# Storing the low parts of the input projection's weights in the first half and loading them in the second

## The chip, the cores and the metric

One core of a Trainium2 chip runs the whole layer. The metric is the device time of one execution in microseconds. TensorE is called PE here, VectorE DVE, ScalarE ACT, GpSimd POOL and SyncE SP; SP issues nearly all of the kernel's DMA transfers, in the order in which they stand in its queue.

## The reference, cut to what matters

One layer of a hybrid encoder, 1024 rows by 1024 channels in fp32. The input projection has 3088 columns that three groups of heads share; the rest of the layer follows from them.

```python
h = rmsnorm(x, pre_mix_norm[l])
proj = h @ w_in[l]
(a_q, a_k, a_v, s_z, s_xbc, s_dt, g_qkv, g_z, g_b, g_a) = jnp.split(proj, offs, axis=-1)
att = swa_sink_alibi(a_q, a_k, a_v, attn_sinks[l])     # sliding window attention
ssd = ssd_mixer(s_z, s_xbc, s_dt, ...)                 # conv, chunked state space scan
gdn = gdn_mixer(g_qkv, g_z, g_b, g_a, ...)             # conv, chunked delta rule with a triangular solve
mix = jnp.concatenate([att, ssd, gdn], axis=-1) @ w_out[l]
x = x + rmsnorm(mix, post_mix_norm[l])
h = rmsnorm(x, pre_ffn_norm[l])
f = (jax.nn.silu(h @ ffn_w_gate[l]) * (h @ ffn_w_up[l])) @ ffn_w_down[l]
x = x + rmsnorm(f, post_ffn_norm[l])
```

## The kernel before, in words

The 1024 rows are worked on in two halves of 512. Each half of phase 1 computes its input projection, the gated delta rule (`gdn_*`), the state space blocks (`ssd_*`) and attention; the second half also holds the out projection of the first half's rows. Phase 2 does the out projection of the second half and the feed-forward part, which the change doesn't touch.

Every fp32 matrix product is made of three products of rounded operands. A weight piece of 128 x 512 (four blocks of 128 x 128, or two of 128 x 256) is loaded from HBM on SP (`wr`, three buffers), ACT rounds it to `hi` (`wh`, six buffers), and a subtract gives the rest, `lo` = raw - `hi` (`wl`, six buffers). PE then multiplies `hi` by `hi`, `hi` by `lo` and `lo` by `hi` into one PSUM tile. `split_eng` gives the subtracts of phase 1 to POOL and DVE in turn. The same weights are loaded, rounded and subtracted in both halves: 48 pieces of the input projection in each, named after their columns (gz for the gate rows, gk, gq, gv, B, C, x, z, aq, ak, av).

The order on each engine isn't written out: a scheduler in the framework sets it from estimated times and from priorities (the code in `tc.high_priority()` goes ahead where it can), and it is fixed when the program is built. Each engine then runs its list in order, and so does SP: a transfer whose data or buffer isn't ready holds up every transfer behind it. SP's transfers use eight completion semaphores in turn, so each also waits for the one eight before it.

Three places are needed below. At the start, the second half's rows of x (tile `x`, line 291) are loaded early, and ACT (`junk`, line 250) and DVE normalise them between the first matmuls of the gate columns (`mm_gz`) and their evacuation (`gth_gz`, `dtn`, `gz`). In each half DVE inverts a unit triangular matrix per chunk (lines 505 to 550): a loop of 16 steps (`Tpr`, `Tst`, lines 521 and 523), the result stored to HBM (`vd<-Tst`, line 525) and loaded back in another layout (`Tst<-vd`, `Wst<-vd`, lines 527 and 528), then two products of four slices each (lines 534 and 536), stored again (line 541) and loaded as `Vd` (line 554) for the matmuls `lx` (line 573). On the same DVE run the conv steps (line 347), the masks `sE` (line 693), which PE needs for `y` (line 700), and the state `ssd_st` (line 714). At the end of phase 1 attention's rows `o` (lines 902 and 904) are transposed (`tp_f`, line 228) for the out projection.

Of the kernel before, what the change touches and what calls it, by code (L numbers as in the profile page):

```python
# [8 lines left out]
F32 = mybir.dt.float32  # L9
F32R = mybir.dt.float32r  # L10
AF = mybir.ActivationFunctionType
ALU = mybir.AluOpType
# [4 lines left out]
P = 128  # L17
SEQ = 1024
D = 1024
KB = D // P  # L20
# [10 lines left out]
WC = 544  # L31
# [38 lines left out]
def trunk(ctx, tc, a):  # L70
    nc = tc.nc
    dma = nc.sync.dma_start
# [4 lines left out]
    def f32(ap):  # L77
        return ap.bitcast(F32)
# [4 lines left out]
    dpool = ctx.enter_context(tc.tile_pool(name="dpool", bufs=1, space=DRAM))  # L83
# [86 lines left out]
    def split_eng():  # L170
        cnt[0] += 1
        return pool if phase[0] == 1 and cnt[0] % 2 else vec

    def split_piece(name, n, width, hi, lo, fill):

        def v(t):
            return t[:, 0:n * width].rearrange("p (k c) -> p k c", k=n)

        with tc.high_priority():
            raw = wpool.tile([P, WC], F32, tag="wr", name=f"wr_{name}")  # L180
            for dst, src in fill:
                dma(v(raw)[:, :, dst:dst + src.shape[1]], src.rearrange("(k p) c -> p k c", p=P))
            act(out=v(hi), in_=v(raw), func=AF.Copy)  # L183
            split_eng().tensor_tensor(v(lo), v(raw), f32(v(hi)), op=ALU.subtract)  # L184
        return [(v(hi)[:, k], v(lo)[:, k]) for k in range(n)]

    def wpair(name):
        return [wsp.tile([P, WC], F32R, tag=tg, name=f"{tg}_{name}") for tg in ("wh", "wl")]

    def piece(name, srcs, kb, width=P, tiles=None):  # L190

        out = []
        n0 = WC // width
        for k0 in range(0, kb, n0):
            n = min(n0, kb - k0)
            nm = f"{name}{k0}"
            out += split_piece(nm, n, width, *(tiles or wpair)(nm),
                               [(dst, src[k0 * P:(k0 + n) * P]) for dst, src in srcs])
        return out

    def gemm_rows(ps, hl, wp, tsl):

        for k, ((hi, lo), (whi, wlo)) in enumerate(zip(hl, wp)):
            pe.matmul(ps, hi[:, tsl], whi, start=k == 0, stop=False)  # L204
            pe.matmul(ps, hi[:, tsl], wlo, start=False, stop=False)  # L205
            pe.matmul(ps, lo[:, tsl], whi, start=False, stop=k == len(wp) - 1)  # L206

    def gemm(ps, wp, hl):
        for k, ((whi, wlo), (hi, lo)) in enumerate(zip(wp, hl)):
            pe.matmul(ps, whi, hi, start=k == 0, stop=False)  # L210
            pe.matmul(ps, whi, lo, start=False, stop=False)  # L211
            pe.matmul(ps, wlo, hi, start=False, stop=k == len(wp) - 1)  # L212
# [105 lines left out]
        return hT  # L318

    def proj(h, hT, name, parts):  # L320
        wp = piece(f"{name}{h}", parts, KB)
        ps = ps_mm.tile([P, HT], F32, tag="mm", name=f"mm_{name}{h}")
        gemm(ps, wp, hT)
        return ps

    def proj_rows(h, hT, name, parts, width, evac):

        wp = piece(f"{name}{h}", parts, KB, width)
        for t in range(NT):
            ps = ps_mm.tile([P, HT], F32, tag="mm", name=f"mm_{name}{h}{t}")  # L330
            gemm_rows(ps[:, 0:width], hT, wp, slice(t * P, (t + 1) * P))
            evac(t, ps)

    def conv_block(h, hT, name, col, b, out):
        ps = proj(h, hT, name, [(0, w_in[:, col:col + P])])
        cb = cpool.tile([P, HT + 3], F32, tag="cb", name=f"cb_{name}{h}")
        if h == 0:
            pool.memset(cb[:, 0:3], 0.0)
        else:
            pool.tensor_copy(cb[:, 0:3], carry[:, b, :])  # L340
        act(out=cb[:, 3:], in_=ps, func=AF.Copy)
        if h == 0:
            pool.tensor_copy(carry[:, b, :], cb[:, HT:HT + 3])
        u = out
        act(out=u, in_=ps, func=AF.Identity, scale=wconv[:, b, 3:4], bias=wconv[:, b, 4:5])
        for i in (2, 1, 0):
            stt(out=u, in0=cb[:, i:i + HT], scalar=wconv[:, b, i:i + 1], in1=u,
                op0=ALU.mult, op1=ALU.add)
        th = cb[:, 0:HT]
        act(out=th, in_=u, func=AF.Tanh)  # L350
        stt(out=out, in0=th, scalar=1.0, in1=u, op0=ALU.add, op1=ALU.mult)

    def gate_rows(h, hT, name, parts, width, more=None):

        out = [ablk(f"{name}{h}{i}") for i in range(2)]
        tiles = [out[t // 2][:, t % 2 * 256:(t % 2 + 1) * 256] for t in range(NT)]

        def evac(t, ps):
            th = cpool.tile([P, HT + 3], F32, tag="cb", name=f"gth_{name}{h}{t}")[:, 0:256]
            act(out=th, in_=ps[:, 0:256], func=AF.Tanh, scale=0.5)  # L360
            stt(out=tiles[t], in0=th, scalar=1.0, in1=ps[:, 0:256], op0=ALU.add, op1=ALU.mult)
            if more is not None:
                more(t, ps)

        proj_rows(h, hT, name, parts, width, evac)
        return tiles
# [421 lines left out]
    def half(h, hT, order):  # L788
# [35 lines left out]
        def att_blocks():  # L824
            aq = []
            for b in range(2):
                ps = proj(h, hT, f"aq{b}", [(0, w_in[:, b * 64:b * 64 + 64]),
                                            (64, w_in[:, 128 + b * 64:192 + b * 64])])
                aq.append(ablk(f"aq{h}{b}"))
                act(out=aq[b], in_=ps, func=AF.Copy)  # L830
            ps = proj(h, hT, "ak", [(0, cols(O_AK))])
            ak = ablk(f"ak{h}")
            act(out=ak, in_=ps, func=AF.Copy)
            ps = proj(h, hT, "av", [(0, cols(O_AV))])
            avT = cpool.tile([P, HT + 3], F32, tag="cb", name=f"avT{h}")[:, 0:HT]
            act(out=avT, in_=ps, func=AF.Copy)
            ps = mx(f"tp_av{h}")
            for t in range(NT):
                pe.transpose(ps[:, t * P:(t + 1) * P], avT[:, t * P:(t + 1) * P], ident)
            av = ablk(f"av{h}").rearrange("p (t c) -> p t c", t=NT)  # L840
            act(out=av, in_=ps.rearrange("p (t c) -> p t c", t=NT), func=AF.Copy)
            st["att"] = (aq, ak, av)
# [17 lines left out]
    def block_first():  # L860
# [14 lines left out]
        for g in range(ng):  # L875
            c0 = g * gw
            wp = piece(f"wo{h}{g}", [(0, a["w_out"][0][:, c0:c0 + gw])], KB, gw)
            for t in range(NT):
                r0 = h * NT + t
# [221 lines left out]
    for g in range(2):  # L1101
        ps = [mx(f"mm_o1{g}{t}", ("f", ("mm", "tp")[t % 2])[g]) for t in range(NT)]
        if g == 0:
            for t in range(NT):
# [3 lines left out]
        wp = {k: piece(f"wo1{g}{k}", [(0, a["w_out"][0][k * P:(k + 1) * P, g * HT:(g + 1) * HT])], 1, HT)[0]  # L1108
              for k in korder}
# [244 lines left out]
```

## Time and profile before

| | |
|---|---|
| time, median of 3 runs | 1271.78 us (1269.67 to 1272.04) |
| profiled execution, time | 1269.6 us |
| profiled execution, span | 1267.8 us |
| mean granted clock of TensorE | 0.983 |
| busy: PE, DVE, ACT, POOL | 1217.6, 924.2, 573.6, 214.6 us |
| moved by DMA | 168.15 MB; HBM read 126.82, written 40.11 MB |

Times inside the execution count from the span's start. Phase 1's first half runs to about 200 us, its second half to about 560 us. A row of the timeline gives start and duration in us, engine, line, operation and tiles, and in brackets the engine's idle time before it with what ended it. A row of the waits gives the total, the number and the longest.

### The profile page before, as it was taken

Reading aid. Unit: us, or ns where it says so; the run is one execution under the profiler, and the core shown is the slowest. Engines: PE = TensorE matmul, PEld = TensorE weight load, DVE = VectorE, ACT = ScalarE, POOL = GpSimd, SP = SyncE. Lnnn points to the kernel's source line nnn. Section 1 sums busy time; section 2 is a strip of 40 time slices with the busy share of each in tenths; the row PEclk is TensorE's granted clock in tenths of the full one; section 3 lists DMA queues with packets and bytes.
Section 4 is the critical chain, followed back from the end, with each engine's and each line's share of the span. In section 5 each row is a group of like instructions: output and inputs, shape, how many; then the busy total and the mean of one; then the engine's idle time right before and its main releaser. Section 6 shows DMA issues by size and latency. Waiting matters only on the chain.

```text
span 1267.8 us, 18690 instructions
## 1 busy us (share of the span) xinstructions
PE 1217.6 (96%) x6432; PEld 1008.5 (80%) x6432; DVE 924.2 (73%) x1850; ACT 573.6 (45%) x1245; POOL 214.6 (17%) x313
## 2 busy tenths in 40 slices
PE   4999999999998999979999999999999999999997
PEld 4878788887787889867887888888888887888885
DVE  5677875887788585654577999886677767767885
ACT  7454434546444353553456344333333334444661
POOL 3343454333444531200010000000000000000000
PEclk9999999999998999979999999999999999999999
DMA  7323433133332213458263465442333368676315
GB/s 228 97 71 70 91 74 81 53 107 85 82 82 58 87 41 115 127 191 271 77 224 106 159 210 174 160 155 84 125 108 108 106 230 286 184 234 212 96 57 199
DMA packets 181795, 168.15 MB, mean 133 GB/s; under 512 B 52510, under 2 KB 137018, under 8 KB 181700
## 3 DMA queue, kind: packets, MB, share of 16 engines
q1 hardware_dynamic: 164276, 133.14, 35.9%
q10 hardware_dynamic: 17424, 33.82, 7.2%
q8 instruction: 50, 0.82, 0.3%
q14 instruction: 45, 0.37, 0.1%
HBM read 126.82 MB, written 40.11 MB: 132 GB/s over the span
## 4 chain that ended last, share of the span: by engine, by line
PE 81%; DVE 9%; DMA 4%; ACT 2%; issue 2%; SPq 1%; POOL 1%; ACTq 0%; DVEq 0%; POOLq 0%
PE mm_p L1225 5%; PE mm_p L1227 5%; PE mm_p L1226 5%; PE gram L486 1%; PE mm_o L1118 1%; PE mm_o L1119 1%; PE mm_o L1120 1%; PE ao L779 1%; PE mm_o L204 1%; PE y L700 1%; DVE Tpr L534 1%; PE mm_o L205 1%; PE mm_o L206 1%; DMA x<-in_x_dram 1%; DMA wr_e<-in_ffn_w_gate_dram 1%
## 5 line engine op out<-in xcount | busy, mean ns | idle before, releaser
L167 POOL TENSOR_TENSOR rsq<-ssv,mhalf 128x1 f32<-128x1 f32 x32 | 20.8, 654 | 745.0 <-DVE ssv L257 714.8
L183 ACT ACTIVATE wh_wo<-wr_wo 128x512 fp32r<-128x512 f32 x32 | 19.9, 630 | 41.5 <-DMA wr_wo<-in_w_out_dram 16.5
L204 PE MATMUL mm_z<-wh_z,hhi_a 128*128 128x256 f32 x128 | 38.4, 300 | 0.0
L184 DVE TENSOR_TENSOR wl_wo<-wr_wo,wh_wo 128x512 fp32r<-128x512 f32 x24 | 17.6, 733 | 27.9 <-ACT wh_wo L183 27.6
L204 PE MATMUL mm_o<-wh_wo,hhi_m 128*128 128x256 f32 x128 | 37.0, 289 | 0.0
L205 PE MATMUL mm_z<-wl_z,hhi_a 128*128 128x256 f32 x128 | 36.7, 287 | 0.0
L206 PE MATMUL mm_z<-wh_z,hlo_a 128*128 128x256 f32 x128 | 36.6, 286 | 0.0
L205 PE MATMUL mm_o<-wl_wo,hhi_m 128*128 128x256 f32 x128 | 35.7, 280 | 0.0
L206 PE MATMUL mm_o<-wh_wo,hlo_m 128*128 128x256 f32 x128 | 35.7, 280 | 0.0
L1118 PE MATMUL mm_o<-wh_wo,mhi 128*128 128x512 f32 x64 | 25.2, 394 | 1.4 <-ACT mhi L233 1.4
L210 PE MATMUL mm_x<-hhi_a,wh_x 128*128 128x512 f32 x64 | 26.1, 408 | 0.0
L700 PEld LDWEIGHTS y<-xs,sE 128*128 128x128 f32 x128 | 18.9, 201 | 9.0 <-DVE sE L693 7.4
L211 PE MATMUL mm_x<-hlo_a,wh_x 128*128 128x512 f32 x64 | 25.9, 404 | 0.0
L700 PE MATMUL y<-xs,sE 128*128 128x64 f32 x128 | 19.8, 284 | 6.3 <-DVE sE L693 6.3
L212 PE MATMUL mm_x<-hhi_a,wl_x 128*128 128x512 f32 x64 | 25.8, 403 | 0.0
L204 PEld LDWEIGHTS mm_z<-wh_z,hhi_a 128*128 128x128 f32 x128 | 25.3, 197 | 0.6
L1119 PE MATMUL mm_o<-wl_wo,mhi 128*128 128x512 f32 x64 | 25.2, 393 | 0.0
L205 PEld LDWEIGHTS mm_z<-wl_z,hhi_a 128*128 128x128 f32 x128 | 24.9, 195 | 0.3
L206 PEld LDWEIGHTS mm_z<-wh_z,hlo_a 128*128 128x128 f32 x128 | 25.0, 196 | 0.0
L1120 PE MATMUL mm_o<-wh_wo,mlo 128*128 128x512 f32 x64 | 24.5, 396 | 0.0
L204 PEld LDWEIGHTS mm_o<-wh_wo,hhi_m 128*128 128x128 f32 x128 | 24.1, 188 | 0.4 <-issue 0.3
L205 PEld LDWEIGHTS mm_o<-wl_wo,hhi_m 128*128 128x128 f32 x128 | 24.0, 188 | 0.3 <-issue 0.3
(1623 smaller groups left out, 4379.2 us busy)
## 6 DMA issues: line engine op xcount, KB each, us to landing
wr_wo<-in_w_out_dram SPq DMA_DIRECT2D x32, 256.0 KB
x<-in_x_dram SPq DMA_DIRECT2D x8, 512.0 KB
wr_x<-in_w_in_dram SPq DMA_DIRECT2D x16, 256.0 KB
wr_z<-in_w_in_dram SPq DMA_DIRECT2D x16, 256.0 KB
res<-in_x_dram SPq DMA_DIRECT2D x8, 512.0 KB
resf<-x1d SPq DMA_DIRECT2D x8, 512.0 KB
mixn<-mixd SPq DMA_DIRECT2D x12, 256.0 KB
wr_e<-in_ffn_w_gate_dram SPq DMA_DIRECT2D x12, 256.0 KB
```

What stands on the lines that cost most here:

```text
L204: pe.matmul(ps, hi[:, tsl], whi, start=k == 0, stop=False)
L205: pe.matmul(ps, hi[:, tsl], wlo, start=False, stop=False)
L206: pe.matmul(ps, lo[:, tsl], whi, start=False, stop=k == len(wp) - 1)
L210: pe.matmul(ps, whi, hi, start=k == 0, stop=False)
L211: pe.matmul(ps, whi, lo, start=False, stop=False)
L700: pe.matmul(yd[:, j], E[:, j, :], xs[:, j], start=True, stop=True)
L1118: pe.matmul(ps[t], hi[:, s], whi, start=k == korder[0], stop=False)
L1119: pe.matmul(ps[t], hi[:, s], wlo, start=False, stop=False)
L1120: pe.matmul(ps[t], lo[:, s], whi, start=False, stop=k == korder[-1])
L1225: pe.matmul(ps[j], ah[:, s], bh, start=i == 0, stop=False)
L1226: pe.matmul(ps[j], ah[:, s], bl, start=False, stop=False)
L1227: pe.matmul(ps[j], al[:, s], bh, start=False, stop=i == NP - 1)
```

## The change

The first half computes each `lo` as before and also stores it to a tile in HBM (`low_*`); the second half loads it from there instead of subtracting. Raw load and rounding stay in both halves, and the out projection's pieces keep their subtracts. SP's queue grows from 565 to 661 instructions, POOL's shrinks from 318 to 294 and DVE's from 1852 to 1828; 12.7 MB more are written and as many read.

```diff
+    low = {}
+
-    def split_piece(name, n, width, hi, lo, fill):
+    def split_piece(name, n, width, hi, lo, fill, keep=None):
...
             act(out=v(hi), in_=v(raw), func=AF.Copy)
-            split_eng().tensor_tensor(v(lo), v(raw), f32(v(hi)), op=ALU.subtract)
+            if keep and keep in low:
+                dma(f32(v(lo)), v(low[keep]))
+            else:
+                split_eng().tensor_tensor(v(lo), v(raw), f32(v(hi)), op=ALU.subtract)
+                if keep:
+                    low[keep] = dpool.tile([P, WC], F32, name=f"low_{keep}")
+                    dma(v(low[keep]), f32(v(lo)))
...
-    def piece(name, srcs, kb, width=P, tiles=None):
+    def piece(name, srcs, kb, width=P, tiles=None, keep=None):
...
-                               [(dst, src[k0 * P:(k0 + n) * P]) for dst, src in srcs])
+                               [(dst, src[k0 * P:(k0 + n) * P]) for dst, src in srcs], keep and f"{keep}{k0}")
...
-        wp = piece(f"{name}{h}", parts, KB)
+        wp = piece(f"{name}{h}", parts, KB, keep=f"{name}_")
...
-        wp = piece(f"{name}{h}", parts, KB, width)
+        wp = piece(f"{name}{h}", parts, KB, width, keep=f"{name}_")
```

The scheduler orders everything anew. In the changed program the subtract is line 189, the load of a low part line 187, its store line 192, and what stands behind is 8 lines further on (L525 is L533).

SP's queue at the start, around the last two loads of the second half's x. Before (`vd<-S_bd` stores zeros):

```order
L955 DMA vd_138<-S_bd 16x16x16 x3
L182 DMA wr_gq_649<-in_w_in_dram 128x4x128
L955 DMA vd_138<-S_bd 16x16x16
L182 DMA wr_gq_655<-in_w_in_dram 128x4x128
L182 DMA wr_gk_696<-in_w_in_dram 128x4x128
L291 DMA x_2735<-in_x_dram 128x1024
L291 DMA x_2737<-in_x_dram 128x1024
L153 DMA cw_gdn_364<-in_gdn_conv_w_dram 4x384
```

Now:

```order
L184 DMA wr_gq_661<-in_w_in_dram 128x4x128
L192 DMA low_gz_430<-wl_gz_424 128x544
L184 DMA wr_gq_669<-in_w_in_dram 128x4x128
L184 DMA wr_gk_712<-in_w_in_dram 128x4x128
L299 DMA x_2831<-in_x_dram 128x1024
L192 DMA low_gk_0_614<-wl_gk_609 128x512
L192 DMA low_gk_4_622<-wl_gk_617 128x512
L299 DMA x_2833<-in_x_dram 128x1024
```

Three stores of low parts now stand among these transfers, two of them between the two loads of x; the four small stores of zeros have moved behind x.

SP's queue in the second half, around the round trip of the triangular inverse through HBM. Before:

```order
L182 DMA wr_x_4916<-in_w_in_dram 128x4x128
L525 DMA vd_139<-Tst_3737 64x16x16
L182 DMA wr_z_4958<-in_w_in_dram 128x2x256
L525 DMA vd_139<-Tst_3737 64x16x16
L527 DMA Tst_3737<-vd_139 64x8x16 x2
L182 DMA wr_z_4964<-in_w_in_dram 128x2x256
L528 DMA Wst_3731<-vd_139 64x16x16 x2
```

Now:

```order
L187 DMA wl_x_4964<-low_x_4_2213 128x512
L184 DMA wr_z_5054<-in_w_in_dram 128x2x256
L533 DMA vd_139<-Tst_3833 64x16x16 x2
L184 DMA wr_z_5060<-in_w_in_dram 128x2x256
L187 DMA wl_x_5005<-low_x_0_2257 128x512
L535 DMA Tst_3833<-vd_139 64x8x16
L536 DMA Wst_3827<-vd_139 64x16x16
L187 DMA wl_x_5011<-low_x_4_2265 128x512
L184 DMA wr_z_5066<-in_w_in_dram 128x2x256
L535 DMA Tst_3833<-vd_139 64x8x16
L536 DMA Wst_3827<-vd_139 64x16x16
```

One low load stands between the store and the first load back, and a low load and a raw load between the two loads of Tst.

DVE in the same place, from the first product to the second set of masks. Before:

```order
L534 TENSOR_TENSOR Tpr_3739<-Tst_3737,Wst_3731 128x512
L721 TENSOR_SCALAR y_4603<-y_4603,rsq 128x256
L184 TENSOR_TENSOR wl_x_4915<-wr_x_4916,wh_x_4914 128x512
L536 TENSOR_REDUCE Wst_3731<-Tpr_3739 128x32
L347 SCALAR_TENSOR_TENSOR B_4766<-cb_B_4804,wconv,B_4766 128x512
L534 TENSOR_TENSOR Tpr_3739<-Tst_3737,Wst_3731 128x512
L347 SCALAR_TENSOR_TENSOR B_4766<-cb_B_4804,wconv,B_4766 128x512
L536 TENSOR_REDUCE Wst_3731<-Tpr_3739 128x32
```

Now:

```order
L729 TENSOR_SCALAR y_4699<-y_4699,rsq 128x256
L355 SCALAR_TENSOR_TENSOR B_4862<-cb_B_4900,wconv,B_4862 128x512 x2
L542 TENSOR_TENSOR Tpr_3835<-Tst_3833,Wst_3827 128x512
L355 SCALAR_TENSOR_TENSOR B_4862<-cb_B_4900,wconv,B_4862 128x512
L544 TENSOR_REDUCE Wst_3827<-Tpr_3835 128x32
L701 SCALAR_TENSOR_TENSOR sE_4716<-sE_4716,sp_3394,tp_x_4727 128x128 x4
L542 TENSOR_TENSOR Tpr_3835<-Tst_3833,Wst_3827 128x512
```

The subtract has gone from between the products, and the scaling of y and two conv steps of B stand ahead of the first product.

## The prediction

> **What bounds the kernel now.** I read the busy shares of the page first, then TensorE's (PE's) waits, then busy time by stretch of 20 us (columns: PE, weight loads, DVE, ACT, POOL, granted clock, DMA share, GB/s).
>
> ```profile
> span 1267.8 us, 18690 instructions
> PE 1217.6 (96%) x6432; PEld 1008.5 (80%) x6432; DVE 924.2 (73%) x1850; ACT 573.6 (45%) x1245; POOL 214.6 (17%) x313
> ```
> ```profile
> PE y L700 <- DVE sE L693: 6.3, 2, 3.9
> PE tp_f L228 <- ACT o L902: 4.1, 1, 4.1
> PE tp_f L228 <- DVE o L904: 4.0, 1, 4.0
> PE mm_gz L204 <- ACT dtn L375: 0.8, 1, 0.8
> ```
> ```profile
> 40.00:134.00 94.00, 94.00 (x471) 74.53 (x470) 73.66 (x163) 47.43 (x103) 35.98 (x61) 1.00 0.34 83
> 230.00:340.00 110.00, 110.00 (x682) 89.45 (x682) 85.83 (x231) 56.87 (x147) 39.47 (x57) 1.00 0.29 81
> 380.00:400.00 20.00, 15.35 (x78) 12.91 (x77) 20.00 (x33) 7.50 (x18) 9.47 (x10) 0.87 0.31 69
> 420.00:520.00 100.00, 99.61 (x838) 90.84 (x837) 62.57 (x177) 41.49 (x119) 31.81 (x47) 1.00 0.25 80
> 540.00:560.00 20.00, 11.82 (x81) 10.98 (x80) 11.78 (x30) 11.76 (x28) 2.17 (x4) 0.76 0.53 164
> ```
>
> PE works 96% of the span, and from 40 to 134, 230 to 340 and 420 to 520 us it never rests. What is taken from DVE or POOL there is worth nothing, because PE's own work sets the pace. So the change can move the end only where PE waits: the start, the two stretches in which PE waits for the masks sE (one in each half), and the tail of phase 1 near 550. In 380 to 400 DVE is busy for all 20.00 us: there DVE is the bound.
>
> **Term 0: the subtracts themselves.** These are the groups of line 184 (min/median/max in ns, first and last start).
>
> ```profile
> L184 POOL TENSOR_TENSOR wl_z<-wr_z,wh_z x8: 1288/1463/1757, 95.5 to 378.9; 128x512 fp32r<-128x512 f32 x8
> L184 DVE TENSOR_TENSOR wl_z<-wr_z,wh_z x8: 670/690/693, 102.1 to 387.6; 128x512 fp32r<-128x512 f32 x8
> L182 SPq DMA_DIRECT2D wr_z<-in_w_in_dram x16: 367/390/850, 82.4 to 373.0; - x16
> ```
>
> The second half loses 48 subtracts: 24 on DVE at 0.69 us (16.6 us) and 24 on POOL at 1.46 us (35 us). SP gains 96 transfers of 256 KB; their issue at 0.39 us is 19 us a half, on a queue that mostly stands idle. Where PE never rests the removal is worth 0; the work that hides it is PE's matmuls. A store delays only the reuse of its low tile, six pieces on. A piece feeds 12 matmuls, at 94.00 us for 471 records 0.20 us apiece, so six pieces are at least 14 us, against 0.39 us of issue and 0.7 us on the engines (256 KB at the 359 GB/s of term 1's last row): 0, between 0 and +1. The loads have the same slack where PE is the bound: 0, between 0 and +1.
>
> **Term 1: the start, a loss.** The second half's x tiles are loaded at 24 us, and ACT and DVE normalise them ahead of emptying the first gate matmuls, so PE ends up behind x.
>
> ```profile
> 24.05 0.93 SPq L291 DMA_DIRECT2D x<-in_x_dram  x2
> 29.15 0.63 ACT L250 ACTIVATE junk<-x 128x512 bf16<-128x512 f32 x1 [2.35 <-DMA x<-in_x_dram]
> 31.07 0.63 ACT L250 ACTIVATE junk<-x 128x512 bf16<-128x512 f32 x1 [0.45 <-DMA x<-in_x_dram]
> 35.13 0.39 PE L204 MATMUL mm_gz<-wh_gz,hhi_a 128*128 128x272 f32 x1 [0.77 <-ACT dtn L375]
> 26.00:28.00 2.00, 0.64 (x1) 0.13 (x1) 2.00 (x6) 0.62 (x2) 0.00 (x0) 0.52 1.06 359
> ```
>
> The DMA engines are full here (share 1.06 at 359 GB/s). The new order puts one stored gate piece (278 KB) ahead of these two x tiles and two stored gk pieces (512 KB) between them, and four small vd stores behind them. The two stores cost 2 x 0.39 = 0.8 us of issue; 0.52 MB at 359 GB/s is 1.5 us, all 0.8 MB 2.2 us. I take 2.1 us later for the last x, because the share is over 1 there: the PE wait grows from 0.77 to 2.9 us. Whether the clock then halves is read from the other waits, in windows of 2 us (PE busy, clock, DMA share, GB/s):
>
> ```profile
> 154.65 0.50 PE L440 MATMUL D_s<-mask_r,ident_r 128*128 128x512 f32 x1 [1.75 <-DVE ssd_st L714]
> 156.00:158.00 2.00, 2.00 (x8) 0.50 0.04 8
> 158.00:160.00 2.00, 2.00 (x11) 0.70 0.60 128
> 164.62 0.95 PE L700 MATMUL y<-xs,sE 128*128 128x64 f32 x6 [2.42 <-DVE sE L693]
> 396.00:398.00 2.00, 2.00 (x9) 0.50 0.01 4
> 398.00:400.00 2.00, 2.00 (x8) 0.50 0.38 94
> 400.00:402.00 2.00, 2.00 (x13) 0.61 0.13 37
> ```
>
> After a wait of 1.75 us two windows run at 0.50 and 0.70: 2 x (1 - 0.50) + 2 x (1 - 0.70) = 1.6 us lost on top of the wait; after the 3.91 us that term 3 shows, 1.0 + 1.0 + 0.8 = 2.8 us. The wait of 0.77 has no such row behind it. So 2.1 + 1.6 = **+3.7 us**; bounds +1 (the stores find gaps and the clock holds) and +6 (2.8 us late and the clock loses 2.8).
>
> The Trainium skill ("TensorE: Matmul & The Clock Gate", Part 1) says that the clock falls to half after at least one idle window of about 3.4 us. By that a wait of 2.9 us would leave the clock alone and the term would be +2.1; this trace has it fall after 1.75 us, so the trace decides. The skill ("DMA: Bandwidth & Descriptors", Queues, rings and completion order) also says that each DMA engine takes one queue's descriptors in ring order: a store issued before x goes before x, which speaks against the change; no row of this trace holds a store ahead of a load that PE waits for, so none bears it out yet.
>
> **Term 2: the first half's mask wait.** DVE inverts a triangular factor: a loop of 16 steps, then T goes to HBM (vd), comes back (Tst, Wst), then two products whose reduces share DVE with conv and masks.
>
> ```profile
> 134.14 1.34 SPq L525 DMA_DIRECT2D vd<-Tst  x2
> 138.75 0.67 SPq L527 DMA_DIRECT2D Tst<-vd  x1
> 141.77 1.06 DVE L534 TENSOR_TENSOR Tpr<-Tst,Wst 128x512 f32<-128x512 f32 x1 [2.48 <-DMA Tst<-vd]
> ```
>
> All subtracts stay here, and four stores enter SP's queue around this round trip, with a store waiting for its own subtract just ahead of each vd row. The product starts some 2 to 3 us later (two or three transfers of 256 KB at 0.39 + 0.7 us each); against that the new DVE order does two conv steps and four masks before it. PE waits 1.75 + 2.42 us in this place, each with some 1.6 us of clock loss. Bounds: -5 (one of the waits gone with its clock) to +3 (the whole delay on PE). I take **+0.8**, nearer the loss, since the only thing added here is work on SP.
>
> **Term 3: the second half's mask wait, the gain.**
>
> ```profile
> 362.95 0.62 SPq L525 DMA_DIRECT2D vd<-Tst  x1
> 365.48 1.28 SPq L527 DMA_DIRECT2D Tst<-vd  x2
> 366.91 0.62 ACT L183 ACTIVATE wh_x<-wr_x 128x512 fp32r<-128x512 f32 x1
> 369.08 1.06 DVE L534 TENSOR_TENSOR Tpr<-Tst,Wst 128x512 f32<-128x512 f32 x1 [1.89 <-DMA Tst<-vd]
> 387.56 0.67 DVE L184 TENSOR_TENSOR wl_z<-wr_z,wh_z 128x512 fp32r<-128x512 f32 x1
> 388.16 1.51 DVE L716 TENSOR_TENSOR y<-y,z 128x256 f32<-128x256 f32 x1
> 395.07 1.10 DVE L693 SCALAR_TENSOR_TENSOR sE<-sE,sp,tp_x 128x128 f32<-128x128 f32 x4
> 395.46 1.97 PE L700 MATMUL y<-xs,sE 128*128 128x64 f32 x8 [3.91 <-DVE sE L693]
> 401.87 1.30 SPq L541 DMA_DIRECT2D vd<-Tst  x2
> 406.01 0.37 SPq L554 DMA_DIRECT2D Vd<-vd  x1
> 411.02 0.69 PE L573 MATMUL lx<-T,Wn 32*32 32x32 f32 x16
> ```
>
> From the product's start to sE, DVE takes 26.0 us. Three subtracts leave (at 0.67 us or more, 2.0 to 2.5 us); DVE time stretched beside POOL's subtracts shrinks by 1 to 2 us (L716 takes 1.51 here, over twice a subtract of double its size); and two conv steps and a scaling of y, sized like the subtracts (3 x 0.7 us), move ahead of the product: some 19.5 to 21 us remain. But the product itself starts later. The new SP order puts two low loads and one weight load between the two halves of Tst<-vd; that weight load waits for ACT's rounding at 366.91, done 367.53. So the second Tst goes out at about 368 instead of 366.1 and the product starts near 371 (bounds 370, if ACT rounds sooner, and 374, if the burst of three raw and four low loads, 7 x 0.7 us, also delays vd). Then sE comes at 390.5 to 392, where PE arrives at 391.5 (395.46 - 3.91): the wait shrinks from 3.91 to 0 to 1 us, and with it goes the clock loss of 2.8 us. That is 3.4 + 2.8 = 6.2 us won.
>
> What is late next: lx. It hangs on the end of the second product: vd<-Tst, Vd<-vd 4.14 us behind it, and at most 5.0 us from there to lx. sE to vd<-Tst took 6.8 us; a subtract and some y work leave it, so vd<-Tst goes out near 396 and lx is ready between 402 and 405. PE comes there earlier than before: the new order has lx after 25 fewer matmuls (at 0.12 us, 99.61 for 838, 3 us), so at 391.5 + 15.6 - 2.8 - 3 = 401. The wait of 1 to 4 us there gives 1 to 3 back, since other matmuls are late only once. Term 3 is **-4**, bounds -7 (no wait at either place) and 0 (product at 374).
>
> **Term 4: the tail.** PE rests 8.2 us in 540 to 560, on the o rows of attention; 16 subtracts of w_out stay as they are, DVE's order there differs little: **-0.5**, between -1 and +3.
>
> **Sum:** 3.7 + 0.8 - 4 - 0.5 = 0.0. The profiled execution took 1269.6 us, 2.2 under the median of 1271.78; on the median's basis 1271.8. A measurement tells about 0.2% (2.5 us) from no change.
>
> **The rivals.**
> (a) *Faster*: the product starts at 370, lx is ready in time (-7), the first half's order helps (-2.5), and x is only 1 us late (+1): -8.5, 1263 us. For it: the DVE-bound row 20.00 of 20. Against: the vd round trip, which waits for DMA (1.89 us) and not for DVE.
> (b) *Slower*: the round trip itself decides. In both halves vd, Tst and Wst stand behind 256 KB transfers; with a product start of 374 in the second half DVE's saving is eaten up (0 instead of -4), and the same delay costs +2 in the first half; the other terms as summed, that is 3.7 + 2 - 0.5 = +5.2, or 1277 us. It decides from a product start of about 372.5 on, where a microsecond later is one microsecond more and the half clock is back. For it: the full DMA engines at the start, and the issue order. Against: the second half's DMA share of 0.31.
> (c) *Hidden at the start*: the stores slip into the half-empty time before 24 us and the clock holds: +1 instead of +3.7, the rest as summed: 1269.
> (d) *By the skill's clock rule*: waits under 3.4 us cost no clock, so term 1 is +2.1 and the sum -1.6, 1270. The rows at 156 and 166 us speak against it: 1 in 20.
>
> **How the numbers follow.** The sum as it stands (1269.5 to 1274): 0.35, mostly no measurable change. (b) 0.30. (a) 0.20. (c) 0.10. (d) 0.05. The last two lie at the border of a gain, as do the ends of the sum's own case. Faster: 0.20 + half of (c) + 0.06 of the first = 0.31; slower: 0.30 + 0.06 = 0.36; same 0.33. Range: from just above (a), which takes the best bound of every term, to (b) with term 1 nearer its upper bound: 1264 to 1279.
>
> **What would show it.** Term 1: ACT's junk rows on the last x after 31.07, PE's wait in front of mm_gz above 0.77, and a clock below 1.00 behind it. Term 2: the L534 product after 141.77 plus term 1, waits of 1.75 and 2.42 larger or gone. Term 3: PE's wait for sE under 1 us and no half clock near 396; a new wait in front of lx; DVE under 20.00 of 20. Term 4: the tp_f waits within a microsecond. The forecast is wrong if low loads make PE wait in a stretch where it never rests, or if the stores hold back raw weights.

## The result, and the profile after

The changed kernel is slower by about 0.36%: 1275.76 us median of 9 runs (1272.73 to 1279.12) against 1271.49 (1269.40 to 1273.37), a ratio of 1.0036 with a 95% interval of 1.0021 to 1.0051. A second set of 12 runs gave 1275.04 against 1270.86, ratio 1.0031 (1.0019 to 1.0043). The profiled execution took 1272.73 us, 3.0 under that kernel's median, so the traces differ by 3.2 us of span (1267.8 before) where the medians differ by 4.3.

Busy shares on the page after:

```profile
span 1271.0 us, 18771 instructions
PE 1219.4 (96%) x6432; PEld 1009.7 (79%) x6432; DVE 896.2 (71%) x1826; ACT 574.1 (45%) x1245; POOL 180.4 (14%) x289
```

DVE gave up 28 us and POOL 34, and PE's work stayed. What moved is where PE waits:

```profile
PE y L708 <- DVE sE L701: 4.1, 2, 2.4
PE mm_gz L212 <- ACT dtn L383: 3.3, 1, 3.3
PE tp_f L236 <- ACT o L910: 3.1, 1, 3.1
PE tp_f L236 <- DVE o L912: 2.9, 1, 2.9
PE tp_p L776 <- ACT asc L767: 2.3, 3, 1.7
PE tp_x L693 <- DVE y L723: 1.5, 1, 1.5
PE lx L581 <- DVE T L569: 1.4, 1, 1.4
```

The wait for sE, both halves together, shrank from 6.3 to 4.1 us, and the wait behind x grew from 0.8 to 3.3. The waits for lx and for attention's scores (tp_p) are new at this size.

Three marks on PE show where the time went. They are the first start of mm_gk (end of the start), the last start of gram (the second half's first block of work done) and the first start of e00p (end of phase 1). The two starts in a row, in us, stand behind the three times of one matmul in ns. The first three rows are of the kernel before, the last three of the changed one:

```profile
L210 PE MATMUL mm_gk<-hhi_a,wh_gk x32: 388/393/481, 41.8 to 289.8; 128*128 128x512 f32 x32
L486 PE MATMUL gram<-kq x64: 376/376/480, 65.2 to 334.6; 64*128 64x256 f32 x64
L927 PE MATMUL e00p<-hhi_m,wh_e00w x8: 392/398/776, 560.9 to 568.0; 128*128 128x512 f32 x8
```
```profile
L218 PE MATMUL mm_gk<-hhi_a,wh_gk x32: 387/393/398, 46.0 to 293.7; 128*128 128x512 f32 x32
L494 PE MATMUL gram<-kq x64: 376/376/480, 69.4 to 338.9; 64*128 64x256 f32 x64
L935 PE MATMUL e00p<-hhi_m,wh_e00w x8: 388/393/775, 565.3 to 572.9; 128*128 128x512 f32 x8
```

From these rows and the same ones of every other profile, in us:

| profile | start to mm_gk | to last gram | to e00p | to the end | median, ratio to before (95%) |
|---|---|---|---|---|---|
| before | 41.8 | 292.8 | 226.3 | 706.9 | 1271.49 |
| before again | 43.2 | 292.9 | 224.6 | 707.5 | 1271.02, 1.0007 (0.9990 to 1.0023) |
| changed | 46.0 | 292.9 | 226.4 | 705.7 | 1275.76, 1.0036 (1.0021 to 1.0051) |
| changed again | 46.1 | 293.2 | 226.3 | 706.0 | 1275.04, 1.0031 (1.0019 to 1.0043) |
| only gz, gk | 46.7 | 291.9 | 225.9 | 704.5 | 1273.55, 1.0026 (1.0011 to 1.0040) |
| stores late | 44.6 | 292.0 | 223.7 | 705.3 | 1267.16, 0.9968 (0.9955 to 0.9980) |
| stores late again | 44.0 | 292.1 | 222.6 | 706.7 | 1267.64, 0.9984 (0.9963 to 1.0004) |
| loads only | 44.8 | 297.5 | 223.3 | 706.2 | 1268.68, 0.9995 (0.9974 to 1.0016) |
| no gz, gk | 41.9 | 294.6 | 224.1 | 705.6 | 1270.76, 0.9995 (0.9981 to 1.0009) |
| before, new order | 44.8 | 294.2 | 229.4 | 707.3 | 1273.43, 1.0019 (1.0003 to 1.0034) |
| changed, new order | 45.6 | 294.8 | 224.1 | 707.2 | 1275.15, 1.0044 (1.0026 to 1.0063) |
| stores late, new order | 41.5 | 293.6 | 222.2 | 706.4 | 1269.03, 0.9991 (0.9976 to 1.0007) |
| stores only | 46.2 | 294.1 | 226.8 | 708.2 | 1276.15, 1.0029 (1.0014 to 1.0043) |
| stores late, tail | 43.2 | 295.9 | 222.5 | 705.6 | 1265.06, 0.9963 (0.9947 to 0.9979) |

The ratios are taken within each batch, where the kernel before had medians of 1270.44 to 1271.54 us; they are not quotients of the medians. Each row is one execution, and the half clock alone moves a stage by some us between two profiles of one program (41.8 and 43.2 us for the start of the kernel before), so a stage is only read where several rows agree. The marks don't cut equal work out of programs of different order. The last column is phase 2, which no term of the theory touches: it ran from 704.5 to 708.2 us, so some 3 us of any total can come from there.

### The profile page after: what moved, and what is told of

It is laid out like the page before. It is cut to its first block, busy times and chain, and to the rows that moved or that the text cites. A ratio compares the mean times of both kernels' runs of the same rounds, so it can differ in the third digit from the quotient of the medians.

```text
span 1271.0 us, 18771 instructions
## 1 busy us (share of the span) xinstructions
PE 1219.4 (96%) x6432; PEld 1009.7 (79%) x6432; DVE 896.2 (71%) x1826; ACT 574.1 (45%) x1245; POOL 180.4 (14%) x289
## 3 DMA queue, kind: packets, MB, share of 16 engines
q1 hardware_dynamic: 178100, 158.45, 41.9%
## 4 chain that ended last, share of the span: by engine, by line
PE 84%; DVE 6%; DMA 5%; ACT 2%; issue 1%; SPq 1%; POOL 1%; ACTq 0%; DVEq 0%; POOLq 0%
PE mm_p L1233 5%; PE mm_p L1234 5%; PE mm_p L1235 5%; PE gram L494 1%; PE mm_o L1126 1%; PE mm_o L1127 1%; PE mm_o L1128 1%; PE as L751 1%; DMA x<-in_x_dram 1%; PE mm_o L212 1%; PE mm_o L213 1%; PE ao L787 1%; PE y L708 1%; DMA yb<-in_ffn_w_down_dram 1%; PE mm_o L214 1%
## 5 line engine op out<-in xcount | busy, mean ns | idle before, releaser
L212 PE MATMUL mm_gz<-wh_gz,hhi_a 128*128 128x272 f32 x64 | 21.8, 341 | 5.2 <-ACT dtn L383 3.3
L214 PEld LDWEIGHTS mm_o<-wh_wo,hlo_m 128*128 128x128 f32 x128 | 24.9, 194 | 0.0
```

## Experiments

The theory after the result: the stores ahead of x lose 3 to 4 us at the start; the loads win about 5 at the second half's mask wait; the tail gives that back, because the scheduler placed an attention tile differently. The first rival was that the 25 MB of added transfers slow PE wherever they run.

**Only gz and gk.** The suffix of the stored name decides:

```diff
-... keep and f"{keep}{k0}")
+... keep and keep[:2] in ("gz", "gk") and f"{keep}{k0}")
```

> Only the gz and gk pieces (8 of 48) are stored and loaded; SP's order at the start is that of the changed kernel, the tail's order on PE that of the kernel before. Theory (the start, by stores ahead of x, costs about 4 us; the rest of the change cancels): PE waits about 3 us in front of the third gate matmul group, a half clock follows, the time is 3 to 5 us over the kernel before (ratio 1.003). Rival (the added HBM traffic costs PE everywhere, in proportion): 8 of 48 pieces, under 1 us over.

Ratio 1.0026, some 3 us: 8 of 48 pieces bring most of the loss. The profile shows the wait at its place, and the mask wait of the second half untouched (in this section the rows of waits count those from 300 to 600 us):

```profile
PE y L708 <- DVE sE L701: 3.9, 1, 3.9
37.73 0.59 PE L212 MATMUL mm_gz<-wh_gz,hhi_a 128*128 128x272 f32 x1 [3.66 <-ACT dtn L383]
```

**Stores late.** The store is moved out of the block of high priority:

```diff
                 split_eng().tensor_tensor(v(lo), v(raw), f32(v(hi)), op=ALU.subtract)
-                if keep:
-                    low[keep] = dpool.tile([P, WC], F32, name=f"low_{keep}")
-                    dma(v(low[keep]), f32(v(lo)))
+        if keep and keep not in low:
+            low[keep] = dpool.tile([P, WC], F32, name=f"low_{keep}")
+            dma(v(low[keep]), f32(v(lo)))
```

> All 48 pieces stored and loaded, but the stores are issued without the high priority, so that SP's order at the start has x ahead of them as in the kernel before. Theory: the start is back to that of before (first gk matmul near 41.8 us instead of 46.0), the second half's mask wait is still shorter by about 6 us with its clock loss, the tail depends on its new order on PE: in all 4 to 8 us under the changed kernel, 0 to 4 under the kernel before. Rival (HBM traffic): stays 4 us over the kernel before, since the bytes are the same.

1267.16 us (6 runs), ratio 0.9968: under the kernel before, with every byte of the added traffic. That ends the first rival. PE's wait behind x is 1.30 us here instead of 3.26, though mm_gk came at 44.6 us and not near the expected 41.8:

```profile
36.44 0.40 PE L212 MATMUL mm_gz<-wh_gz,hhi_a 128*128 128x272 f32 x1 [1.30 <-ACT dtn L383]
```

**Loads only.** One tile is stored (key av_0), and the second half's pieces other than gz load that tile, so their low parts are not their own:

```diff
-            if keep and keep in low:
-                dma(f32(v(lo)), v(low[keep]))
+            if keep and h_of(name) == 1 and keep[:2] != "gz":
+                dma(f32(v(lo)), v(low["one"]))
...
-                if keep:
+                if keep == "av_0":
```

`h_of` returns the half that is being built.

> Nothing but one tile is stored late in the first half, and 44 of the second half's pieces load that one tile as their low part instead of subtracting (gz still subtracts); the low parts are so not the right ones. Theory: start and first half as in the kernel before; the second half's mask wait shorter by about 6 us; the tail's order is nearly that of the changed kernel and gives some 4 to 5 us back: 0 to 3 us under the kernel before. Rival (the gain in the second half is not from the loads): no change at the mask wait, and slower by the tail, 3 to 5 us over.

Ratio 0.9995 (0.9974 to 1.0016). The wait for sE in the second half fell to 1.56 us, so the shorter wait comes with the loads. The total stayed within noise, and its one profile, 5 us over this kernel's median, doesn't show the tail as the reason: from the last gram to e00p it took 223.3 us against 226.3 and 224.6 before, and it lost 4.7 us ahead of that, under a half clock that the last section shows.

**No gz and gk**, the complement of the first (`not in` for `in`):

> The 40 pieces other than gz and gk are stored and loaded; gz and gk subtract in both halves. Theory: start as before, first half +0.5, second half's mask wait shorter by about 6 us, the tail by its own new order (two attention tiles reach past the last out projection matmuls): 0 to 4 us under the kernel before. Rival (HBM traffic): 40 of 48 pieces, some 3.5 us over.

Ratio 0.9995 (0.9981 to 1.0009), within what the theory allowed and far from the rival's 3.5 us. Start 41.9 us, wait for sE 2.18, and new waits of 8.7 us for attention's scores in the tail:

```profile
PE tp_p L776 <- ACT asc L767: 8.7, 3, 4.3
PE y L708 <- DVE sE L701: 2.4, 2, 2.2
```

**A program order that holds the tail.** If the first two attention tiles stand ahead of the out projection, the end of phase 1 on PE reads the same in all three, the kernel before, the changed one and the one with late stores: all attention, 48 out projection matmuls, 16 transposes.

```diff
-       "K V G0 G1 G2 G3 S0 s00 s01 s02 s03 S1 s10 s11 s12 s13 A O a0 a1 a2 a3")
+       "K V G0 G1 G2 G3 S0 s00 s01 s02 s03 S1 s10 s11 s12 s13 A a0 a1 O a2 a3")
```

> The kernel before, with the first two attention tiles of the second half ahead of the first half's out projection in the program (A a0 a1 O a2 a3), so that the end of phase 1 on PE reads all attention, 48 out projection matmuls, 16 transposes, as in the kernel before. A control for the next two: by both theories within 3 us of the kernel before, the mask waits and the start unchanged.

> The changed kernel with the same new program order; its last attention tile now stands ahead of the last 48 out projection matmuls. Theory (the changed kernel's tail lost 3 to 5 us by the order of that tile): against the control, start +4, second half -5 to -6, tail 0: 1 to 3 us under the control. Rival (the tail is set by the attention chain whatever the order, and takes back what the mask wait gains): start +4, and the sum of second half and tail 0: 4 us over the control.

> Late stores (as in the second experiment) and the same new program order. Theory: start 0, second half -5 to -6, tail 0: 4 to 7 us under the control and faster than every kernel so far. Rival: 0 to 3 us under the control.

The control came to 1273.43, the changed kernel to 1275.15, late stores to 1269.03. By the profiles the theory holds: from the last gram to e00p 229.4 us for the control, 224.1 and 222.2 for the two with loads, so here the gain gets through against the control, though not clearly against the kernel before (226.3 and 224.6). By the medians it holds for late stores (4.4 us under the control) and not for the changed kernel: 1.7 over the control, where the theory said 1 to 3 under and the rival 4 over. The control's profile was its longest execution (1277.53 us against a median of 1273.43), so its 229.4 is too long for its own median. This test is undecided on the size: between the two expectations. Two of its results speak against the order of the attention tile as the whole matter. The control is slower than the kernel before (1.0019), and the held tail did not make late stores faster, though that was expected: 0.9991, against 0.9968 and, below, 0.9984 without it.

**Stores only**: the second half subtracts again.

```diff
-            if keep and keep in low:
-                dma(f32(v(lo)), v(low[keep]))
-            else:
+            if True:
                 split_eng().tensor_tensor(v(lo), v(raw), f32(v(hi)), op=ALU.subtract)
-                if keep:
+                if keep and keep not in low:
```

> The first half stores its 48 low parts, the second half doesn't load them and subtracts as before. Theory: the start costs 3 to 4 us, the first half's mask wait 0 to +1, the second half's mask wait stays at 3.9 us with its half clock, the tail has its own new order (0 to +4): 3 to 8 us over the kernel before. Rival (stores are free and the loss comes with the loads): within 1 us of the kernel before.

1276.15 us, ratio 1.0029: the stores alone, with no gain to set against them, are as slow as the whole change. The mask wait is back, and a wait for the scores is in the tail:

```profile
PE y L706 <- DVE sE L699: 4.4, 1, 4.4
PE tp_f L234 <- ACT o L908: 2.9, 1, 2.9
PE tp_p L774 <- ACT asc L765: 2.8, 1, 2.8
```

**The two kernels and late stores once more**, for a second profile each:

> The kernel before once more, as its own control: a second profile of it, and how far two sets of runs of one program lie apart. Every theory: ratio 1.000 within 0.0015; if its first gk matmul comes at another time than 41.8 us, the start's length varies from run to run by the clock alone.

> The changed kernel once more: a second profile and a second ratio. Theory: ratio 1.002 to 1.005; PE's wait in front of the third gate matmul group near 3.3 us again, while the kernel before has 0.8; the mask wait of the second half near 2 us with no half clock; the tail's tp_f waits as before. Rival (the profile's start was an accident of the clock): first gk matmul within 1 us of that of the kernel before in the same batch.

> Late stores once more (all 48 pieces stored and loaded). Theory: 0.996 to 0.999 of the kernel before, 5 to 8 us under the changed kernel in the same batch. Rival (its first result was luck of six runs): within 2 us of the kernel before or above it.

Both kernels came out as before; late stores at 0.9984 (0.9963 to 1.0004), this time within noise of the kernel before, though clear of the changed one. The last x arrives at the same time in both profiles of each kernel (rows of before again, then of changed again):

```profile
30.80 0.63 ACT L250 ACTIVATE junk<-x 128x512 bf16<-128x512 f32 x1 [0.23 <-DMA x<-in_x_dram]
35.00 0.59 PE L204 MATMUL mm_gz<-wh_gz,hhi_a 128*128 128x272 f32 x1 [1.43 <-ACT dtn L375]
```
```profile
33.84 0.63 ACT L258 ACTIVATE junk<-x 128x512 bf16<-128x512 f32 x1 [1.36 <-DMA x<-in_x_dram]
37.90 0.60 PE L212 MATMUL mm_gz<-wh_gz,hhi_a 128*128 128x272 f32 x1 [3.09 <-ACT dtn L383]
```

**Late stores and a tail with one attention tile past the out projection, not two:**

```diff
-                att_tile(h, t, kv, *st["att"], att_prev[0])
+                with tc.high_priority() if h == 1 and t >= NT - 2 else nullcontext():
+                    att_tile(h, t, kv, *st["att"], att_prev[0])
```

> Late stores, and high priority for the last two attention tiles of the second half, so that on PE only one of them, not two, reaches past the start of the last 48 out projection matmuls. Theory (the tail's order costs what the mask wait gains): 1 to 4 us under the late stores of the same batch. Rival (the tail is set by something else): within 1 us of it.

1265.06 us, ratio 0.9963 (0.9947 to 0.9979): 2.6 us under late stores by the medians, as the theory said, though the two intervals overlap; the means of the 12 runs each differ by 3.3 us, with a 95% interval of 0.2 to 6.4. The marks don't show it: from the last gram to e00p this profile took 222.5 us against 223.7 and 222.6. Idle time and clock loss over the last 50 us ahead of e00p, added up in windows of 2 us, did fall, from 18.5 and 17.8 us to 15.9, but the 105 us behind the last gram, with the mask wait, lost 2 us more here (6.2 against 4.3 and 3.9). It is the fastest kernel of this study, 5.8 us under the kernel before and 10 under the changed one.

## Why the prediction was right and where it was wrong

The forecast was 1271.8 us, range 1264 to 1279; the result lies in the range, 4 us above the point, and with 15 us of width that says little. The case of the sum (1269.5 to 1274, chance 0.35) did not come; slower had 0.36. It was slower by another mechanism than rival (b): the round trip through HBM did not swallow DVE's saving. One term was wrong, the tail. Terms 1 and 3 came out near their sums, each in part by luck, as shown below. The range also wasn't what it was called: rival (a) doesn't take the best bound of every term, which would be 1 - 5 - 7 - 1 = -12 us.

By the marks the changed kernel differs from the kernel before, in the first and the second pair of profiles, by +4.2 and +2.9 us at the start, +0.1 and +0.3 to the last gram, +0.1 and +1.7 to e00p, and -1.2 and -1.5 in phase 2. The prediction has no term for phase 2, which the scheduler also ordered a little differently; why it is shorter stays open.

*Term 1, the start (+3.7 predicted).* Right in its path, and near in size. The last x came 2.7 us later (33.74 against 31.07), PE waited 3.26 us in front of mm_gz instead of 0.77, and a half clock follows:

```profile
25.50 1.10 SPq L192 DMA_DIRECT2D low_gk<-wl_gk  x2
26.69 0.86 SPq L299 DMA_DIRECT2D x<-in_x_dram  x1
33.74 0.63 ACT L258 ACTIVATE junk<-x 128x512 bf16<-128x512 f32 x1 [1.08 <-DMA x<-in_x_dram]
37.80 0.40 PE L212 MATMUL mm_gz<-wh_gz,hhi_a 128*128 128x272 f32 x1 [3.26 <-ACT dtn L383]
38.00:40.00 2.00, 2.00 (x10) 0.52 0.86 153
```

The delay comes from SP's issue and hardly from the bytes. The issue of the last x ended at 27.55 us (26.69 + 0.86) against 24.98 before (24.05 + 0.93), so 2.6 of the 2.7 us were lost by the end of its issue. The prediction gave 0.8 us to the issue of the two stores between the loads and the rest of its 2.1 to the bytes; that the sum came out near was luck.

mm_gk starts at 45.6 to 46.7 us in the five profiles whose gz and gk stores are issued early and at 41.5 to 44.8 in the nine others; the means are 46.1 and 43.3. So the term is +2.8 on average, and +4.2 and +2.9 in the two pairs. Most of it is the wait: mm_gz behind it starts at 37.7 us on average in the five and at 35.4 in the nine. The half clock isn't the change's alone. It follows this wait in all five, and also in six of the nine, among them the kernel before in its second profile (first row: before, second: before again, where the wait was 1.43 us):

```profile
36.00:38.00 2.00, 2.00 (x18) 1.00 0.00 0
36.00:38.00 2.00, 2.00 (x11) 0.50 0.00 0
```

So the 1.6 us of clock loss in the term are about 0.5 on average. Rival (c), that it is hidden, fell. On rival (d): waits of 3.0 to 3.7 us are near the 3.4 us at which the Trainium skill ("TensorE: Matmul & The Clock Gate", Part 1) has the clock fall anyway, so these rows don't tell the two apart; the half clock behind 1.75 us still does, and so do those six, behind waits of 1.30 to 2.45 us. The other three waited 0.73 to 1.07 us and kept the clock. The Trainium skill ("DMA: Bandwidth & Descriptors", Queues, rings and completion order) states that a DMA engine takes a queue's descriptors in ring order; these rows don't test it, since nearly all of the delay is in the issue.

*Term 2, the first half (+0.8).* From mm_gk to the last gram 292.8 and 292.9 us before, 292.9 and 293.2 after: +0.2. The product did start later (148.70 against 141.77, 2.7 of it beyond the 4.2 of the start), but y, which waits for the masks, only 2.2 later (166.82 against 164.62):

```profile
148.70 1.05 DVE L542 TENSOR_TENSOR Tpr<-Tst,Wst 128x512 f32<-128x512 f32 x1 [3.12 <-DMA Tst<-vd]
158.71 0.41 PE L693 MATMUL tp_x<-cst,x 128*128 128x128 f32 x2 [1.53 <-DVE y L723]
166.43 1.11 DVE L701 SCALAR_TENSOR_TENSOR sE<-sE,sp,tp_x 128x128 f32<-128x128 f32 x4
166.82 1.31 PE L708 MATMUL y<-xs,sE 128*128 128x64 f32 x8 [2.40 <-DVE sE L701]
```

The wait of D_s (1.75 us) gave way to one of tp_x (1.53), behind which the clock held, so one of the two half clocks is gone, 1.7 us of loss. The stretch is no shorter for it, which these rows don't explain.

*Term 3, the second half's mask wait (-4).* Right in sum and path, though not in each part:

```profile
373.75 0.58 SPq L535 DMA_DIRECT2D Tst<-vd  x1
376.76 1.05 DVE L542 TENSOR_TENSOR Tpr<-Tst,Wst 128x512 f32<-128x512 f32 x1 [3.33 <-DMA Tst<-vd]
395.97 1.12 DVE L701 SCALAR_TENSOR_TENSOR sE<-sE,sp,tp_x 128x128 f32<-128x128 f32 x4
396.37 1.21 PE L708 MATMUL y<-xs,sE 128*128 128x64 f32 x8 [1.73 <-DVE sE L701]
407.31 0.69 PE L581 MATMUL lx<-T,Wn 32*32 32x32 f32 x16 [1.43 <-DVE T L569]
398.00:400.00 2.00, 2.00 (x18) 1.00 0.36 107
```

The product starts 7.7 us later than before, 4.3 of them carried along (the last gram at 338.9 against 334.6); the other 3.4 compare with 1.9 predicted, and put it at 372.5 us on the times of the kernel before, where rival (b) was to begin. From it to sE DVE needs 19.2 us instead of 26.0 (19.5 to 21 predicted), which kept (b) away. The wait is 1.73 (0 to 1 predicted), the half clock is gone, and lx waits 1.43 us (1 to 4 predicted). That the clock held is luck by the prediction's own row, in which it fell behind a wait of 1.75 us. It held again in the second profile of the changed kernel, behind 1.40 us, but of the seven other profiles with loads in this stretch six had a half clock here, behind waits of 1.56 to 2.18 us, at a loss of 1.6 to 3.3 us. Over the stretch, idle time and clock loss together (rows of before, then after):

```profile
335.00:440.00 105.00, 100.35 (x649) 0.97 0.35 80
515.00:600.00 85.00, 72.77 (x415) 0.90 0.62 197
```
```profile
335.00:440.00 105.00, 101.46 (x666) 1.00 0.54 138
515.00:600.00 85.00, 73.89 (x403) 0.86 0.57 186
```

4.65 + 0.03 x 105 = 7.8 us before and 3.5 after: -4.3. In windows of 2 us, the second pair of profiles gives the same (7.9 and 3.6).

*Term 4, the tail (-0.5): the step that failed.* From the last gram to e00p the two kernels take the same: 226.3 and 224.6 before, 226.4 and 226.3 after. With -4.3 in the mask stretch the tail must have lost 4 to 6 us. The second rows above show a lower clock there, 0.86 against 0.90 over 85 us (3.4 us more lost to half the clock), while PE rests no longer, 11.1 us against 12.2. So the loss stands in the clock: in windows of 2 us over the last 50 us ahead of e00p it took 4.8 and 1.3 us before and 8.2 and 8.0 after, and idle time 10.2 and 11.6, then 10.1 and 9.9. The timeline of the changed kernel shows the place; the row in the fence behind it is of the kernel before:

```profile
543.42 1.00 PE L787 MATMUL ao<-av,apT 128*128 128x64 f32 x8
546.10 0.33 PE L776 MATMUL tp_p<-cst,asc 128*128 128x128 f32 x1 [1.67 <-ACT asc L767]
546.20 0.35 PE L212 MATMUL mm_o<-wh_wo,hhi_m 128*128 128x256 f32 x1
546.00:550.00 4.00, 3.90 (x21) 0.58 0.02 5
```
```profile
543.41 0.35 PE L204 MATMUL mm_o<-wh_wo,hhi_m 128*128 128x256 f32 x1
```

The last 48 out projection matmuls stand behind a transpose of the last attention tile, which waits 1.67 us for ACT's scores; four transposes and twelve small attention matmuls (as, ao) that PE did earlier in the kernel before stand around it. PE came to this place 1.3 us earlier than before (ao at 536.21 against 537.54) and left it 2.8 later. Then the clock was 0.58 from 546 to 550 us, and the 48 matmuls, of which the last starts at 553.3 and started at 549.0 before, took 1.5 us longer. Behind mm_o hangs a serial chain (o, the norm, tp_f) on which PE waits 3 to 4 us twice in either kernel. From the last mm_o to e00p both need 12 us, so each us that mm_o loses is lost at the end. I had read the waits of this chain, and priced the new order as next to nothing because DVE's order there hardly differed. As far as the timeline shows, the order that mattered was PE's, and the term's upper bound of +3 was too low as well.

What is shown and what isn't. That the stores of gz and gk at the start cost about 3 us is shown by two programs that are complements of each other (1.0026 with these pieces alone, 0.9995 with all others) and by the starts of mm_gk. Late stores remove that loss on average: in their four profiles mm_gk starts at 43.3 us (41.5 to 44.6), as in the three of the kernel before and its new order. But of the 5.4 and 6.2 us by which their first two profiles are shorter than those of the changed kernel, only 1.4 and 2.1 lie at the start; 2.7 and 3.7 lie between the last gram and e00p, where their order differs too. That the mask wait shrinks with the loads is shown by every kernel that has them there (1.4 to 2.2 us) and every one that hasn't (3.9 to 4.4). That the tail takes it back is shown by the marks; that it is the order of the attention tile is read from the timeline and supported by the last experiment (2.6 us), and its size isn't settled. With the held tail the last 50 us ahead of e00p lose 16.2 us to idle time and clock in both kernels with loads, 2 less than without it, but the control loses 17.9 there, more than the kernel before (15.1 and 12.9), and the medians of the changed kernel and of late stores with the new order don't fit.

## What to carry to other kernels

A transfer added to a shared queue is priced by what stands behind it at each place, not by its bytes: with all 96 transfers of some 256 KB, but late stores, the kernel was no slower than before, and three stores ahead of one load that PE waited for cost some 3 us. Taking the stores out of the block of high priority was enough to turn a loss of 0.31 to 0.36% into a gain of 0.32%, or 0.16% and within noise the second time. Where a scheduler orders the program, compare the order of the bound engine in every latency-bound stretch, also those that the change doesn't touch: a gain that is made ahead of such a stretch can be lost in it.

## What the runs showed of the hardware that I had not expected

TensorE's clock also fell where PE hardly waited. In the profile of the kernel with loads only, a stretch ran at half the clock for 10.2 us while PE was busy all the time, with small matmuls (32x32 to 128x256) ahead of it; half of that is 5.1 us, and this profile took 4.7 us more than that of the kernel before from mm_gk to the last gram:

```profile
240.00:250.00 10.00, 10.00 (x62) 0.51 0.05 15
250.00:260.00 10.00, 10.00 (x81) 1.00 0.28 92
```

What brought it on is open: the kernel before runs nearly the same row of small matmuls there, from 226 to 240 us, at a clock of 1.00.

The length of a wait alone doesn't tell whether the clock falls behind it. In front of mm_gz it fell from 1.30 us on and held up to 1.07; at the second half's masks it held behind 1.73 us in one program and fell behind 1.56 in another. And the start of one and the same program varies by more than a us (41.8 and 43.2 us before mm_gk), with the clock behind mm_gz at 1.00 in one profile and at 0.50 in the other. That is as much as some of the terms of the sum; one profile of each kernel is not enough to size a term of 2 us.
